# Two transformer blocks on one core: when the conditioning products of the second block are computed

## The chip, the core and the metric

The kernel runs on one core of a Trainium2 chip. The core has TensorE (PE: matmuls), VectorE (DVE), ScalarE (ACT), GpSimd (POOL) and SyncE (SP), which here only issues the transfers from HBM. The metric is the device time of one execution in microseconds, the median of several runs.

## What is computed

Both blocks have two layers, 256 tokens and 1024 channels. The first is a transformer with three mixing branches and a squared-ReLU MLP, the second a block of FFN, mixer, FFN, each behind a norm that is modulated by a conditioning vector `c`. That modulation is what the change is about:

```python
cond = jax.nn.silu(c)
for l in range(DEPTH):
    mod = cond @ ada_w[l] + ada_b[l]                 # 1024 -> 9 * 1024
    sh1, sc1, g1, sh2, sc2, g2, sh3, sc3, g3 = jnp.split(mod, N_MOD, axis=-1)
    hn = _modulate(_rms_norm(h, norm_g[l, 0]), sh1, sc1)
    h = h + 0.5 * g1[:, None, :] * _swiglu(hn, ffn1_w_in[l], ffn1_w_out[l])
    hn = _modulate(_rms_norm(h, norm_g[l, 1]), sh2, sc2)
    ...                                              # four mixers, joined as mixed
    h = h + g2[:, None, :] * (mixed @ w_out[l])
    hn = _modulate(_rms_norm(h, norm_g[l, 2]), sh3, sc3)
    h = h + 0.5 * g3[:, None, :] * _swiglu(hn, ffn2_w_in[l], ffn2_w_out[l])
```

## The kernel before

**Weights.** All matmul weights come in one list of chunks (`_plan`), each cut into pieces of 512 KB. SP loads a piece into one of five buffers `raw`; ACT rounds it to `wh`, DVE subtracts to get the rest `wl` (`split_to`), and PE does three matmuls per block of 128x128 (`mm3`). A piece is split three pieces ahead of its use, and loaded five ahead of its split. A piece of 1024 columns is 24 matmuls. A chunk of the FFNs is two pieces.

**Conditioning.** `cond @ ada_w[l]` isn't done on PE. Each layer has 72 columns of 128 values, 24 for each of the three norms (8 of shift, 8 of scale, 8 of gate). For each column a 512 KB slab of `ada_w` is loaded into one of two buffers `ada`, and one DVE instruction multiplies it by `cond` and sums along the row (`ada_step`). I call this a product. There are 144 of them. A step first issues the load for the next product, so that a load runs one product ahead. The DMA can start only when the product two before it has freed the buffer.

**When products go out.** `chunk` does `prog["ada"]` products at each weight chunk, a number that the stages set: 1 in the twelve gate chunks of both layers of the first block, 0 to 2 in its MLP, 1 in FFN1 of the second block's first layer, 2 in FFN2 of that layer. `ada_to(n)` does at once what is missing up to product n. When column 71 of a layer is there, the bias is added for all 72 columns, and `scl` and `hg` (scale and gate) are made for the three norms. All 144 products are done in the first FFN2.

**Who needs them.** Each norm's values are read first by `Shifted` (called by `following` near the end of the stage ahead): ACT rounds the shift columns of `mods` into the last columns of the tiles `xh`, DVE subtracts for the rest. In the mixer `following` stands behind the last token matmuls (`mv`) and ahead of the output projection (tile `mo`), whose input parts `mixh`, `mixl` are finished there: `fp` is a forget-attention softmax, `fpT` its transposed copy on ACT, `fo` the matmul on it, and `mixh`/`mixl` of `fo` the operand of the third and fourth `mo` piece.

**Order.** The program is written in one order, and a tile scheduler then orders each engine's queue; a queue is worked off in order. An instruction that waits holds everything behind it on its engine, on SP the transfers.

Of the kernel before, what the change touches and what calls it, by code (L numbers as in the profile page):

```python
# [15 lines left out]
ALU = mybir.AluOpType  # L16
# [5 lines left out]
L = 2  # L22
# [99 lines left out]
def tile_model(ctx: ExitStack, tc: tile.TileContext, xT: bass.AP, pos: bass.AP, cvec: bass.AP, wst: bass.AP,  # L122
               ada: bass.AP, vec: bass.AP, vec2: bass.AP, wsT: bass.AP, cst: bass.AP,
               msk: bass.AP, ret: bass.AP, outT: bass.AP):
    nc = tc.nc
# [15 lines left out]
    def const(shape, s, dt=F32):  # L141
        t = cp.tile(shape, dt, tag=s, name=s)
        return t
# [39 lines left out]
    def stt(out, in0, s, in1, op0, op1, **kw):  # L183
        nc.vector.scalar_tensor_tensor(out=out, in0=in0, scalar=s, in1=in1, op0=op0, op1=op1, **kw)  # L184
# [4 lines left out]
    def add(out, a, b):  # L189
        tt(out=out, in0=a, in1=b, op=ALU.add)  # L190
# [17 lines left out]
    for i, t in enumerate(subs):  # L208
        first_sub.setdefault(t[0], i)
    raws, split = {}, {}  # L210
    prog = {"raw": 0, "split": 0, "chunk": 0, "fill": 0, "turn": 0, "ada": 0}

    def load_to(s):
        while prog["raw"] < min(s, len(subs)):
# [7 lines left out]
    def split_to(s, ahead=5):  # L222
        while prog["split"] < min(s, len(subs)):
            i = prog["split"]
            load_to(i + ahead)
            _, _, n, cc, _ = subs[i]
            wh = wp.tile([P, SUB_COLS], F32R, tag="wh", bufs=4, name=nm("wh"))
            wl = wp.tile([P, SUB_COLS], F32R, tag="wl", bufs=4, name=nm("wl"))
            src = raws.pop(i)[:, :n * cc]
            nc.scalar.copy(wh[:, :n * cc], src)  # L230
            ins = tt(out=wl[:, :n * cc], in0=src, in1=wh[:, :n * cc].bitcast(F32), op=ALU.subtract)  # L231
            prog["dve"] = ins.ins
            split[i] = (wh, wl)
            prog["split"] += 1
# [3 lines left out]
    def fill():  # L238

        prog["fill"] += 1  # L240
        for g in list(bgs):
            if prog["fill"] >= due[g]:
                step(g)
# [12 lines left out]
    due = {}  # L256
# [8 lines left out]
    def chunk(key, l, k0, kk, c0, cc):  # L265
        j = prog["chunk"]
        assert plan[j] == (key, l, k0, kk, c0, cc), (plan[j], (key, l, k0, kk, c0, cc))
        prog["chunk"] += 1
        for _ in range(prog["ada"]):
            ada_step()  # L270
        s = first_sub[j]
        while s < len(subs) and subs[s][0] == j:
            split_to(s + 3)
            _, k, n, _, _ = subs[s]
            wh, wl = split.pop(s)
            for i in range(n):
                yield k0 + k + i, wh[:, i * cc:(i + 1) * cc], wl[:, i * cc:(i + 1) * cc]
            fill()
            s += 1
# [67 lines left out]
    def vc(n, i=0, k=1):  # L347
        return V[:, VC[n] + i:VC[n] + i + k]
# [165 lines left out]
    mods = [const([P, 72], f"mods{l}") for l in range(L)]  # L514
    scl = [const([P, 24], f"scl{l}") for l in range(L)]
    hg = [const([P, 24], f"hg{l}") for l in range(L)]
# [4 lines left out]
    def ada_load(upto):  # L521
        while ada_n[0] < min(upto, L * 72):
            i = ada_n[0]
            t = wp.tile([P, 1024], F32, tag="ada", bufs=2, name=nm("ada"))
            with tc.issue_after(prog["dma"]):
                nc.sync.dma_start(t, ada[i])
            ada_raw[i] = t
            ada_n[0] += 1

    def ada_step():  # L530
        i = ada_n[1]
        if i >= L * 72:
            return
        ada_n[1] += 1
        ada_load(i + 2)
        l, j = i // 72, i % 72
        w = ada_raw.pop(i)
        stt(w, w, 1.0, cond[0], ALU.mult, ALU.mult, accum_out=mods[l][:, j:j + 1])
        if j == 71:
            add(mods[l], mods[l], vc(f"adab{l}", 0, 72))  # L540
            for q in range(3):
                stt(scl[l][:, 8 * q:8 * q + 8], mods[l][:, 24 * q + 8:24 * q + 16], 1.0, vc(f"ng{l}", 8 * q, 8),
                    ALU.add, ALU.mult)
                nc.vector.tensor_scalar_mul(hg[l][:, 8 * q:8 * q + 8], mods[l][:, 24 * q + 16:24 * q + 24],
                                            1.0 if q == 1 else 0.5)

    def ada_to(n):
        while ada_n[1] < n:
            ada_step()
# [69 lines left out]
    for l in range(L):  # L619
# [27 lines left out]
        for i in range(5):  # L647
            src = b4[i // 2].t[:, (i % 2) * 256:(i % 2) * 256 + 256]
            hi_, lo_, j, g = (cqh, cql, i, "gq") if i < 3 else (ckh, ckl, i - 3, "gkv")
# [262 lines left out]
                    base_table(ins)  # L912
            return f

        prog["ada"] = 1
        for p in range(12):
            proj_pair(4352 + 256 * p, gate_e(p))

        prog["ada"] = 0
        mixed = [u4("mx") for _ in range(2)]  # L920
        mh = Act(8, "mh")
        for n, (y, gg) in enumerate(((ya, ga), (yb, gb), (yc, gc))):
# [45 lines left out]
        def hid_e(b, m):  # L968
# [3 lines left out]
            mul(q_, r_, r_)  # L972
            sub(hid.l(m, 2), q_, hid.h(m, 2).bitcast(F32))

        b4 = [Bank("u1", True) for _ in range(4)]
        gemm([("U", l, 2 * i, 2, 0, 1024) for i in range(4)], h.h, h.l, pair_outs(b4), 7, after={1: nrm2})
        for j in range(4):
# [2 lines left out]
        bd = [Bank("dn", True) for _ in range(4)]  # L980
        for half in range(2):
            for i in (range(4, 8) if half == 0 else range(8, 16)):
                prog["ada"] = min(2, i - 4)
                b = Bank("u2", half == 0)
                gemm([("U", l, 0, 8, 256 * i, 256)], h.h, h.l, pair_outs([b]), 7)
                hid_e(b, 2 * i)
            for m in range(4):
                prog["ada"] = 0 if half and m == 3 else 1
                gemm([("D", l, 8 * k, 8, 256 * m, 256) for k in (2 * half, 2 * half + 1)], hid.h, hid.l,
                     pair_outs([bd[m]]), 31)  # L990
                if half and l == 0:
                    update(m, bd[m], "full", rsm, "mix1", nh)
                elif half:
                    if m == 0:
                        ada_to(72)
                        mul(gfa, vc("final", 0, 8), scl[0][:, 0:8])
                        xa = Shifted(0, 0, lambda k: gfa[:, k:k + 1])
                    update(m, bd[m], "full", rsm)
                    xa.parts(m)
                    dst = t2("sqf")  # L1000
                    for e in range(2):
                        act(dst[:, e * 256:(e + 1) * 256], xk(2 * m + e), AF.Square, scale=vc("final", 2 * m + e))
                    accumulate(1, m, dst)
# [40 lines left out]
    def following(l, i):  # L1044
        l, i = (l, i + 1) if i < 2 else (l + 1, 0)
        if l == L:
            return None
        return Shifted(l, i, lambda k: scl[l][:, 8 * i + k:8 * i + k + 1])

    def gated_update(j, bank, l, i, nxt, part=None):  # L1050
# [15 lines left out]
    def ffn(l, f, i, xa, first=False):  # L1066
        h, r = Act(8, "h"), rcomb if first else rsx
        hid = Act(22, "hid")
        b4 = [Bank("f1", True) for _ in range(4)]
        nrm = normalised(h, l, i, first)  # L1070
        gemm_shift(("F" + f, l, 0, 8, 0, 512), xa, b4, lambda: next(nrm))
        for j in range(2):
            s_, q_ = t1("sg"), t1("sv")
            bg_, bu_ = b4[2 * j], b4[2 * j + 1]
            cg, cu = shift_bias(bg_), shift_bias(bu_)
            mul(s_, bg_.t[:, 0:256], r)
            act(s_, s_, AF.Silu, bias=cg)
            mul(q_, bu_.t[:, 0:256], r)
            stt(q_, q_, cu, s_, ALU.add, ALU.mult)
            hilo(q_, hid.h(j), hid.l(j))  # L1080
        for j in range(20):
            if j == 2:
                prog["ada"] = 1 if first else 2
            if first and j in range(2, 10):
                next(nrm)
            b = Bank("f2", True)
            gemm([("F" + f, l, 0, 8, 512 + 256 * j, 256)], h.h, h.l, pair_outs([b]), 7)
            s_, q_ = t1("sg"), t1("sv")
            ins = act(s_, b.t[:, 0:256], AF.Silu)
            mul(q_, s_, b.t[:, 256:512])  # L1090
            hilo(q_, hid.h(j + 2), hid.l(j + 2))
        if i == 2:
            ada_to(L * 72)
        nxt = following(l, i)
        base_table(ins)
        for m in range(4):
            if m == 2:
                prog["ada"] = 0
            b = Bank("fd", True)
            parts = [("G" + f, l, k, kk, 256 * m, 256) for k, kk in ((0, 8), (8, 8), (16, 6))]  # L1100
            if nxt is None and m == 3:
                gemm(parts[:2], hid.h, hid.l, pair_outs([b]), 21)
                parts = list(chunk(*parts[2]))
                for e in range(2):
                    for k, wh, wl in parts:
                        mm3(b, b.t[:, e * 256:e * 256 + 256], wh[:, e * P:(e + 1) * P], wl[:, e * P:(e + 1) * P],
                            hid.h(k), hid.l(k), k == 21)
                    gated_update(m, b, l, i, nxt, e)
            else:
                gemm(parts, hid.h, hid.l, pair_outs([b]), 21)  # L1110
                gated_update(m, b, l, i, nxt)
        return nxt
# [411 lines left out]
```

## Time and profile before

| | |
|---|---|
| median of 3 runs | 1986.65 us (1985.24 to 1990.67) |
| the profiled execution, its time | 1991.63 us |
| its span, first to last instruction | 1989.9 us |
| PE busy | 1948.8 us, 98% |
| DVE busy | 1485.2 us, 75% |
| granted TensorE clock, mean | 0.994 |

The profiled execution is 1.73 us longer than its span, and 4.98 us above the median of the runs. All times inside a run below are from the start of the span. PE's busy share is no measure of its pace, since matmuls overlap; where it waits is read from its waits, and what a stage takes from when the first matmul of a stage starts.

### The profile page before, as it was taken

The numbers are of one execution on the slowest core, as the hardware profiler recorded it, in microseconds if no ns is written. First come the engines' busy times: TensorE is split into PE (matmuls) and PEld (weight loads), VectorE is DVE, ScalarE is ACT, GpSimd is POOL, SyncE is SP. The second block draws the span as 40 slices with busy tenths as digits, with TensorE's granted clock in tenths as the row PEclk, the third lists the DMA queues.
The fourth block names the chain that finished last, engine by engine and source line by source line (L and its number), as shares of the span: only waits on it lengthen the run. The fifth ranks groups of instructions, "written<-read, shape, count | busy, mean of one in ns | idle before, by whom it ended". The sixth has DMA issues, their size and how long they took to land.

```text
span 1989.9 us, 38234 instructions
## 1 busy us (share of the span) xinstructions
PE 1948.8 (98%) x15570; PEld 1879.0 (94%) x15570; DVE 1485.2 (75%) x2329; ACT 1056.5 (53%) x1590; POOL 85.6 (4%) x86
## 2 busy tenths in 40 slices
PE   8999999999999999999999998999999999899999
PEld 7989999999989999999999986998999999789999
DVE  7878778796678777789877798888575558977553
ACT  5756555354556555455544466644454445665442
POOL 1000020001010010002000000000000000000000
PEclk9999999999999999999999998999999999999999
DMA  7545657896445656887677633388655554335554
GB/s 257 177 157 207 211 177 254 300 324 230 152 149 180 232 173 204 295 297 283 222 274 269 233 117 106 118 311 302 196 165 201 182 179 158 119 109 169 182 171 127
DMA packets 114945, 406.51 MB, mean 204 GB/s; under 512 B 12880, under 2 KB 14672, under 8 KB 114768
## 3 DMA queue, kind: packets, MB, share of 16 engines
q1 hardware_dynamic: 114768, 404.06, 60.3%
q8 instruction: 122, 2.00, 0.4%
q14 instruction: 55, 0.45, 0.1%
HBM read 402.96 MB, written 1.05 MB: 203 GB/s over the span
## 4 chain that ended last, share of the span: by engine, by line
PE 85%; DVE 9%; ACT 2%; issue 2%; DMA 1%; SPq 0%; POOL 0%; POOLq 0%; DVEq 0%; ACTq 0%
PE f L171 22%; PE fd L171 13%; PE pr L171 12%; PE u L171 9%; PE dn L171 9%; PE br L171 3%; DVE wl L231 2%; PE wo L171 2%; DVE cv L184 2%; PE a L171 1%; PE mo L171 1%; PE sbv L171 1%; PE rv L171 1%; PE uq L171 1%; PE z L171 1%
## 5 line engine op out<-in xcount | busy, mean ns | idle before, releaser
L230 ACT CAST wh<-raw 128x1024 fp32r<-128x1024 f32 (+1 forms) x627 | 642.8, 1030 | 662.7 <-PE fd L171 118.0
L231 DVE TENSOR_TENSOR wl<-raw,wh 128x1024 fp32r<-128x1024 f32 (+1 forms) x627 | 756.0, 1211 | 318.2 <-ACT wh L230 316.4
L171 PE MATMUL f<-hh,wl 128*128 128x256 f32 x1280 | 362.2, 283 | 3.1 <-DVE wl L231 3.1
L171 PE MATMUL f<-hl,wh 128*128 128x256 f32 x1280 | 362.3, 283 | 0.8 <-DVE hl L193 0.8
L171 PE MATMUL f<-hh,wh 128*128 128x256 f32 x1280 | 362.2, 283 | 0.8 <-ACT wh L230 0.6
L171 PEld LDWEIGHTS f<-hh,wl 128*128 128x128 f32 x1280 | 245.4, 192 | 4.4 <-DVE wl L231 4.4
L171 PEld LDWEIGHTS f<-hh,wh 128*128 128x128 f32 x1280 | 245.6, 192 | 1.4 <-ACT wh L230 1.4
L171 PEld LDWEIGHTS f<-hl,wh 128*128 128x128 f32 x1280 | 245.7, 192 | 1.2 <-DVE hl L193 1.2
L184 DVE SCALAR_TENSOR_TENSOR ada<-ada,cond 128x1024 f32<-128x1024 f32 x144 | 176.6, 1227 | 70.6 <-DMA ada<-ada_dram 70.2
L171 PE MATMUL fd<-hidh,wh 128*128 128x256 f32 x704 | 199.3, 283 | 0.6 <-DVE x L184 0.6
L171 PE MATMUL fd<-hidl,wh 128*128 128x256 f32 x704 | 199.2, 283 | 0.0
L171 PE MATMUL fd<-hidh,wl 128*128 128x256 f32 x704 | 199.2, 283 | 0.0
L171 PE MATMUL pr<-hh,wh 128*128 128x256 f32 x672 | 194.8, 290 | 0.0
L171 PE MATMUL pr<-hl,wh 128*128 128x256 f32 x672 | 190.0, 283 | 0.0
L171 PE MATMUL pr<-hh,wl 128*128 128x256 f32 x672 | 190.0, 283 | 0.0
L171 PE MATMUL u<-hh,wh 128*128 128x256 f32 x512 | 145.2, 284 | 0.0
L171 PE MATMUL dn<-hidh,wl 128*128 128x256 f32 x512 | 145.0, 283 | 0.0
L171 PE MATMUL u<-hh,wl 128*128 128x256 f32 x512 | 145.0, 283 | 0.0
L171 PE MATMUL dn<-hidh,wh 128*128 128x256 f32 x512 | 144.9, 283 | 0.0
L171 PE MATMUL dn<-hidl,wh 128*128 128x256 f32 x512 | 144.9, 283 | 0.0
L171 PE MATMUL u<-hl,wh 128*128 128x256 f32 x512 | 144.9, 283 | 0.0
L171 PEld LDWEIGHTS fd<-hidh,wh 128*128 128x128 f32 x704 | 135.2, 192 | 0.8 <-DVE x L184 0.8
(475 smaller groups left out, 4452.0 us busy)
## 6 DMA issues: line engine op xcount, KB each, us to landing
raw<-wst_dram SPq DMA_DIRECT2D x599, 512.0 KB, 3.9
ada<-ada_dram SPq DMA_DIRECT2D x144, 512.0 KB, 5.2
raw<-wst_dram SPq DMA_DIRECT2D x22, 256.0 KB, 2.8
raw<-wst_dram SPq DMA_DIRECT2D x4, 390.0 KB, 3.0
R<-ret_dram SPq DMA_DIRECT2D x2, 512.0 KB, 8.9
out_dram<-x SPq DMA_DIRECT2D x8, 128.0 KB, 3.1
C<-cst_dram SPq DMA_DIRECT2D x1, 896.0 KB, 7.1
v<-vec_dram SPq DMA_DIRECT2D x2, 448.0 KB, 4.6
```

The lines of the kernel that those rows point to most:

```text
L171: nc.tensor.matmul(out, lhsT=lhsT, rhs=rhs, start=grp not in self.open, stop=stop, skip_group_check=True)
L184: nc.vector.scalar_tensor_tensor(out=out, in0=in0, scalar=s, in1=in1, op0=op0, op1=op1, **kw)
L230: nc.scalar.copy(wh[:, :n * cc], src)
L231: ins = tt(out=wl[:, :n * cc], in0=src, in1=wh[:, :n * cc].bitcast(F32), op=ALU.subtract)
```

## The change

The bias, `scl` and `hg` are now made for each norm as soon as its 24 columns are there. `prog["ada"]` may be a fraction: what is due is added up per chunk, and a product goes out when it reaches one. The gate chunks send out none; the chunks of the first block's up projection send one in two, FFN1 and FFN2 of the second block one per chunk in both layers. What a norm still lacks when `Shifted` is about to read it is done at once by `ada_to` in `following`.

```diff
@@ chunk
-        for _ in range(prog["ada"]):
+        prog["due"] += prog["ada"]
+        while prog["due"] >= 1.0:
+            prog["due"] -= 1.0
             ada_step()
@@ ada_step
-        if j == 71:
-            add(mods[l], mods[l], vc(f"adab{l}", 0, 72))
-            for q in range(3):
...
+        if j % 24 == 23:
+            q = j // 24
+            mq = mods[l][:, 24 * q:24 * q + 24]
+            add(mq, mq, vc(f"adab{l}", 24 * q, 24))
...
@@ first block
-        prog["ada"] = 1
         for p in range(12):
             proj_pair(4352 + 256 * p, gate_e(p))
 
-        prog["ada"] = 0
...
+        prog["ada"] = 0.5
         b4 = [Bank("u1", True) for _ in range(4)]
...
-                prog["ada"] = min(2, i - 4)
+                prog["ada"] = 0.5
...
-                        ada_to(72)
+                        ada_to(24)
@@ following
+        ada_to(72 * l + 24 * (i + 1))
         return Shifted(l, i, lambda k: scl[l][:, 8 * i + k:8 * i + k + 1])
@@ ffn
-            if j == 2:
-                prog["ada"] = 1 if first else 2
+            prog["ada"] = 1
...
-        if i == 2:
-            ada_to(L * 72)
```

Counted from the program by the loads, which run one product ahead: 45 stand in the first block, 26 in the first layer's FFN1, 2 in the first mixer (where `ada_to` asks for what is missing of the first layer), 24 in the first FFN2 up to its `following` (the last 4 by `ada_to`), 32 from there to the end of the second layer's FFN1, and the last 15 in the second mixer, where `ada_to(144)` asks for everything that is left.

DVE in the second layer's mixer, between the second part of the mix (`mixl` from `co`) and the operand from `fo`. Before:

```order
L193 TENSOR_TENSOR mixl_19813<-co_20648,mixh_19811 128x512
L611 RECIPROCAL rc_20686<-fs_20680 128x2
...
L595 TENSOR_REDUCE mx_20696<-fs_20666 128x1
L193 TENSOR_TENSOR xh_20711<-mods_161,xh_20711 128x3
...
L231 TENSOR_TENSOR wl_20839<-raw_20578,wh_20838 128x1024
...
L231 TENSOR_TENSOR wl_20881<-raw_20619,wh_20880 128x1024
L1247 COPY do_20807<-do_20802 128x256
L193 TENSOR_TENSOR mixl_19812<-fo_20811,mixh_19810 128x256
```

The same place in the changed kernel, from the last free stretch on:

```order
L184 SCALAR_TENSOR_TENSOR ada_20684,mods_161<-ada_20684,cond_1820 128x1024
L231 TENSOR_TENSOR wl_20885<-raw_20574,wh_20884 128x1024
L184 SCALAR_TENSOR_TENSOR ada_20687,mods_161<-ada_20687,cond_1820 128x1024
L184 SCALAR_TENSOR_TENSOR ada_20690,mods_161<-ada_20690,cond_1820 128x1024
...
L184 SCALAR_TENSOR_TENSOR ada_20705,mods_161<-ada_20705,cond_1820 128x1024
L184 SCALAR_TENSOR_TENSOR ada_20708,mods_161<-ada_20708,cond_1820 128x1024
L190 TENSOR_TENSOR mods_161<-mods_161,V 128x24
L184 SCALAR_TENSOR_TENSOR scl_163<-mods_161,V 128x8
...
L193 TENSOR_TENSOR xh_20715<-mods_161,xh_20715 128x3
...
L193 TENSOR_TENSOR mixl_19767<-fo_20815,mixh_19765 128x256
```

Before, the stretch had no products. Now the fifteen tiles ada_20666 to ada_20708 (numbers in steps of three) are worked off here: the first ahead of the softmax of `fs`, two just ahead of `mixl` from `co`, twelve behind it, the last eight with nothing between them. `mixl` from `fo` stands behind all of them.

ACT at the same place. The names are those of the section on the kernel; `wh` is a rounded weight piece. Before:

```order
L404 CAST xh_20711<-mods_161 128x3
...
L230 CAST wh_20838<-raw_20578 128x1024
...
L584 COPY fpT_20761<-tr_20762 128x384
L584 COPY fpT_20761<-tr_20767 128x384
L230 CAST wh_20880<-raw_20619 128x1024
```

And now:

```order
L230 CAST wh_20884<-raw_20574 128x1024
L1244 ACTIVATE dsq_20812<-do_20806 128x256
L406 CAST xh_20715<-mods_161 128x3
L406 CAST xh_20716<-mods_161 128x3
L406 CAST xh_20717<-mods_161 128x2
L585 COPY fpT_20765<-tr_20766 128x384
L585 COPY fpT_20765<-tr_20771 128x384
L202 CAST mixh_19765<-fo_20815 128x256
```

The three casts of the shift columns wait for `mods` with its bias, so for the last product. The copies `fpT` that the matmul `fo` reads stand right behind them.

SP at the same place, in the changed kernel (before, there are only `raw` loads here):

```order
L528 DMA ada_20684<-ada_dram 128x1024
L218 DMA raw_20882<-wst_dram 128x1024
L528 DMA ada_20687<-ada_dram 128x1024
L528 DMA ada_20690<-ada_dram 128x1024
L218 DMA raw_20924<-wst_dram 128x1024
L528 DMA ada_20693<-ada_dram 128x1024
...
L528 DMA ada_20708<-ada_dram 128x1024
L218 DMA raw_20954<-wst_dram 128x1024
```

Each of these `ada` loads waits on DVE for the buffer that the product two before it held; the weight loads stand between and behind them.

## Rows read from the trace of the kernel before

**Rows 1.** The page, busy time of the engines.
```profile
PE 1948.8 (98%) x15570; PEld 1879.0 (94%) x15570; DVE 1485.2 (75%) x2329; ACT 1056.5 (53%) x1590; POOL 85.6 (4%) x86
```
**Rows 2.** The chain of waits, one weight piece: start, duration.
```profile
86.77 2.87 PE pr L171 x24
```
**Rows 3.** The page's groups: busy, mean ns | idle before, releaser.
```profile
L184 DVE SCALAR_TENSOR_TENSOR ada<-ada,cond 128x1024 f32<-128x1024 f32 x144 | 176.6, 1227 | 70.6 <-DMA ada<-ada_dram 70.2
```
**Rows 4.** Waits of PE, first FFN2 (1269 to 1405): total, times, longest.
```profile
PE f L171 <- DVE wl L231: 2.9, 4, 0.8
PE f L171 <- ACT wh L230: 0.6, 1, 0.6
```
**Rows 5.** Waits of PE, second FFN2's first half (1790 to 1922).
```profile
PE nrm L171 <- POOL ssum L371: 1.9, 1, 1.9
```
**Rows 6.** Timeline of PE, first matmuls of f and fd: start, duration, instruction.
```profile
1269.19 0.28 PE L171 MATMUL f<-xh,wh 128*128 128x258 f32 x1
...
1404.81 0.28 PE L171 MATMUL fd<-hidh,wh 128*128 128x256 f32 x1
...
1790.32 0.28 PE L171 MATMUL f<-xh,wh 128*128 128x258 f32 x1
...
1922.02 0.28 PE L171 MATMUL fd<-hidh,wh 128*128 128x256 f32 x1
```
**Rows 7.** A stretch of the first layer's gate chunks: busy by engine, clock, DMA share, GB/s.
```profile
136.00:234.00 98.00, 98.00 (x817) 93.02 (x816) 78.54 (x126) 57.87 (x87) 0.00 (x0) 1.00 0.62 215
```
**Rows 8.** Timeline of DVE, one product in the first FFN2.
```profile
1350.82 1.23 DVE L184 SCALAR_TENSOR_TENSOR ada<-ada,cond 128x1024 f32<-128x1024 f32 x1 [1.14 <-DMA ada<-ada_dram]
1351.97 0.08 DVE L184 DVE_READ_ACCUMULATOR ada<-ada,cond 128x1 f32 x1
```
**Rows 9.** Timeline of SP, behind that product, and in the second mixer.
```profile
1352.09 0.33 SPq L526 DMA_DIRECT2D ada<-ada_dram  x1
...
1744.51 4.01 SPq L218 DMA_DIRECT2D raw<-wst_dram  x4
```
**Rows 10.** The tile ada: its 144 loads.
```profile
DMA to landing us min/median/max: 3.2/5.2/8.3
```
**Rows 11.** DMA issues from 1800 to 1920: count, size, median us to landing.
```profile
raw<-wst_dram SPq DMA_DIRECT2D x40, 512.0 KB, 3.3
```
**Rows 12.** Timeline of DVE, second mixer, last parts.
```profile
1750.95 0.17 DVE L611 RECIPROCAL rc<-fs 128x2 f32<-128x2 f32 x1 [0.44 <-ACT fp L597]
...
1763.29 0.69 DVE L193 TENSOR_TENSOR mixl<-co,mixh 128x512 fp32r<-128x512 f32 x1 [2.76 <-ACT mixh L202]
1764.87 0.17 DVE L611 RECIPROCAL rc<-fs 128x2 f32<-128x2 f32 x1 [0.88 <-ACT fp L597]
...
1765.92 0.35 DVE L193 TENSOR_TENSOR xh<-mods,xh 128x3 fp32r<-128x3 f32 x3
1767.05 1.23 DVE L231 TENSOR_TENSOR wl<-raw,wh 128x1024 fp32r<-128x1024 f32 x1 [0.78 <-ACT wh L230]
```
**Rows 13.** Timeline of DVE, the bias of the second layer.
```profile
1385.52 0.23 DVE L190 TENSOR_TENSOR mods<-mods,V 128x72 f32<-128x72 f32 x1
```
**Rows 14.** Timeline of ACT, second mixer.
```profile
1765.65 0.42 ACT L404 CAST xh<-mods 128x3 fp32r<-128x3 f32 x3
...
1767.95 0.91 ACT L584 COPY fpT<-tr 128x384 f32<-128x384 f32 x2
```
**Rows 15.** Timeline of PE, second mixer.
```profile
1769.39 0.82 PE L171 MATMUL fo<-fpT,vt 128*64 128x256 f32 x8
...
1772.91 0.47 PE L171 MATMUL mo<-mixl,wh 128*128 128x256 f32 x1
```
**Rows 16.** PE by stretches: length, busy, clock, DMA share, GB/s.
```profile
1738.00:1742.00 4.00, 3.17 (x8) 0.57 0.41 131
1752.00:1756.00 4.00, 4.00 (x15) 0.57 0.14 55
```
**Rows 17.** Waits of PE, first FFN1 (945 to 1077).
```profile
PE f L171 <- DVE hl L193: 0.8, 2, 0.6
```

More of the change, by code (lines that the diff above doesn't have):

```diff
@@ L210, in tile_model @@
     raws, split = {}, {}
-    prog = {"raw": 0, "split": 0, "chunk": 0, "fill": 0, "turn": 0, "ada": 0}
+    prog = {"raw": 0, "split": 0, "chunk": 0, "fill": 0, "turn": 0, "ada": 0.0, "due": 0.0}
     def load_to(s):
@@ L538, in ada_step @@
         stt(w, w, 1.0, cond[0], ALU.mult, ALU.mult, accum_out=mods[l][:, j:j + 1])
-        if j == 71:
-            add(mods[l], mods[l], vc(f"adab{l}", 0, 72))
-            for q in range(3):
[L542 to L545, printed above, removed]
+        if j % 24 == 23:
+            q = j // 24
+            mq = mods[l][:, 24 * q:24 * q + 24]
+            add(mq, mq, vc(f"adab{l}", 24 * q, 24))
+            stt(scl[l][:, 8 * q:8 * q + 8], mq[:, 8:16], 1.0, vc(f"ng{l}", 8 * q, 8), ALU.add, ALU.mult)
+            nc.vector.tensor_scalar_mul(hg[l][:, 8 * q:8 * q + 8], mq[:, 16:24], 1.0 if q == 1 else 0.5)
     def ada_to(n):
```

## The prediction

> **What bounds the kernel now.** I read the page's busy times first: PE 98%, DVE 75% [rows 1]. PE's busy share is no pace, so the waits of PE came next, and they are short. The kernel is a stream of weight pieces at 2.87 us each [rows 2], and nothing that a change does on DVE is felt unless PE has to wait for it. So the question is where the products make PE wait now, and where they will.
>
> Now they do so at one place. The group row puts a product at 1227 ns and DVE's idle time ahead of products at 70.6 us [rows 3], but in most stages PE doesn't feel it. In the first FFN2, with two products per chunk, PE waits 2.9 us for `wl` and 0.6 us for `wh` [rows 4]; the same stage of the second layer, without products, has neither [rows 5], and the wait for `nrm` is the same in both. The stage heads say the same with the restarts in it: from the first `f` to the first `fd` it takes 1404.81 − 1269.19 = 135.62 us in the first layer and 1922.02 − 1790.32 = 131.70 us in the second [rows 6]. All that the spreading can give back is the difference, 3.9 us. Taking the products out of the gate chunks gives nothing: of 98 us there PE is busy for all 98 [rows 7].
>
> **What the change adds: the second mixer.** The count in the program leaves 15 loads for the `ada_to(144)` in the second layer's mixer, and DVE, ACT and SP are each worked off in order. Three things then hang on the last product: on DVE the operand `mixl` from `fo`, on ACT the casts of the shift columns with the copies `fpT` behind them, and through these on PE the matmul `fo`. On SP one weight load stands behind the last six `ada` loads, but its buffer is only freed by a `wl` that comes after the products, so it costs nothing by itself. Nothing in PE's queue can go on past `fo`.
>
> How long do the products take? With two buffers they go round: a product with its read-out lasts 1351.97 + 0.08 − 1350.82 = 1.23 us [rows 8], the next load into its buffer goes out at 1352.09, 0.04 us later [rows 9], and when it has landed the buffer's next product can run. For the landing the rows differ. The 144 loads of `ada` took 3.2 to 8.3 us, median 5.2 [rows 10], but these had weight loads issued just ahead of them. Weight loads of the same size that come singly, one per piece, took 3.3 us [rows 11]. In the mixer the weight buffers are full and two `ada` loads alternate, so I take 3.3, with 3.2 and 5.2 as the ends. A turn of two products is 1.23 + 0.04 + 3.3 = 4.57 us.
>
> The Trainium skill has a price for a load as well: "DMA: Bandwidth & Descriptors", section "Anatomy of one DMA", gives a fixed 2.0 us and the bytes over 436 GB/s, which for 512 KB is an estimate of 3.2 us. The trace agrees in its minimum and not in its median. By that price six turns are 0.6 us shorter than by mine.
>
> Now the places, on the clock of the trace before. The first of the fifteen is loaded right behind the weight load at 1744.51 [rows 9] and its product falls where DVE waits 0.44 us ahead of 1750.95 [rows 12]. The second and third are loaded by then or soon after, and fall into the 2.76 us ahead of `mixl` from `co` at 1763.29 [rows 12]: that wait hides them. The second starts 2.6 us ahead of that, at 1760.7, and ends at 1761.9; from there its buffer goes round. Twelve products are left, six turns: the eleventh ends at 1761.9 + 6 × 4.57 = 1789.3, the twelfth follows directly, at least 1.23 us and with its issue some 1.5 us later, 1790.8. Other work stands between the first ones: the softmax's five small instructions, 1.05 us from 1764.87 to 1765.92, two `wl` of 1.23 us, and a few copies [rows 12]. Followed product by product, the turns hide most of it and 1.8 us stay: 1792.6. The bias is 0.23 us [rows 13], so `mods` is there at about 1792.9.
>
> Then the chain starts: casts 0.42 us, the copies `fpT` 0.91 us [rows 14], and two hand-overs of about 0.1 us, so `fo` starts at 1794.5 and not at 1769.39 [rows 15], 25.1 us late. From `fo` to the free stream of `mo` the trace before takes 3.5 us, to 1772.91 [rows 15], with `mixh` and `mixl` in it; that stays, but the four matmuls of the next piece that ran between aren't done yet, 0.5 us. So PE loses 25.6 us. Ends by the landing: 0.6 less at 3.2 us, and 6 × 1.9 = 11.4 more at 5.2 us.
>
> **The clock behind the wait.** In this mixer PE has short waits, and behind them the granted clock is 0.57 over 4 us, twice: at full busy from 1752 to 1756 and nearly so from 1738 to 1742 [rows 16]. That is mostly the lower of its two levels, 1.2 GHz, and costs 0.43 × 4 = 1.7 us each. A wait of 25 us isn't in the trace, so I take one such stretch, 1.7 us; ends nothing (it falls into the chain from `fo` on, which waits for ACT and DVE anyway) and twice as much.
>
> **The smaller places.** (a) The end of the first FFN2: four forced products and the next ones come with the last weight pieces, eight products at about one per piece, the density that costs 3.9 us over 26 products in the same stage now; 3.9 × 8/26 = 1.2 us. Ends: nothing, or 8 × (3.27 − 2.87) = 3.2 us if every product took half a turn with loads of 5.2 us, (5.2 + 1.27 + 0.07)/2 = 3.27 us, against the 2.87 of a piece. (b) The first mixer: one product on the path of `sg` and the softmax, 1.23 us against a wait of 0.44 as in the second mixer; 0.8 us, ends nothing and 2.2 us. (c) FFN1 of the second layer takes 26 products at one per chunk. FFN1 of the first layer carries that now and has no wait for `wl` or `wh`, only 0.8 us for `hl` at its start [rows 17], so nothing. (d) `scl`, `hg` and the bias now run six times and not twice, on eight to 24 columns: 0.2 us each, hidden, as DVE waits at those places.
>
> **The sum.** −3.9 + 25.6 + 1.7 + 1.2 + 0.8 = +25.4 us. Against the profiled execution, 1991.63 us, that is 2017.0 us. The median of the runs is 4.98 us below that execution, so I forecast 1986.65 + 25.4 = 2012 us. Its own range: down by 0.6 + 1.7 + 1.2 + 0.8 = 4.3 us, and some 4 us for the spread of the runs, to 2004; up by 11.4 us and the spread, to 2025.
>
> **The rivals.**
> 1. The loads in the mixer take 5.2 us, as `ada` loads mostly do now [rows 10], for instance since the two weight loads between them go along. For it: that is their median over 144. Against: those medians come from stages in which a weight load goes out with every product, and here there are two weight loads to fifteen. Price 11.4 us more: 2023.5 us.
> 2. The end of the first FFN2 becomes a second stall. There too the casts of the shift columns stand on ACT, ahead of four roundings `wh`, and wait for the last forced product. PE has three split pieces, 8.6 us, in hand; a load of 5.2 us and two products take 7.7 us, so it just holds. If it doesn't, pieces are late by one or two turns: 8 us more, 2020 us.
> 3. The products wait for no load: DVE does them back to back, 1.5 us each. Twelve are then 18 us and the other work between them 5, from 1761.9 to 1784.5; `mods` comes 8 us sooner and the result is 2004 us. Against: with two buffers a load must land between.
> 4. The other side: the mixer hides the products, and only the gain of the first FFN2 is left, 1986.65 − 3.9 + 2.0 for the small places = 1985 us, or 1983 without these. It decides on DVE, at the cast: `mods` must be there by 1768, when `fpT` is copied now [rows 14]. Twelve products in the 6 us from 1761.9 is 0.5 us each, under half of what one takes on DVE [rows 8]. Only an order of the queues other than the built one could do it.
>
> That the change does not do what its words say is in the forecast: one product per chunk is too few to be done in time, and the rest isn't spread but forced.
>
> **Chances.** Forecast 0.71, rival 1 0.15, rival 2 0.07, rival 3 0.03, rival 4 0.03, and 0.01 for no change. A measurement of this kernel can tell 0.3%, 6 us, from no change; all but the last two are slower by more, so slower 0.96, same 0.01, faster 0.03. The range of 8 in 10, 2004 to 2025 us, holds the forecast with its bounds and rivals 1 and 2 for the most part.
>
> **What would show it.** In the profile after: PE waiting for ACT's `fpT` at `fo` in the second mixer for 20 us or more in one piece, with DVE waiting for DMA `ada` ahead of eight products in a row; starts of products some 4.6 us apart by pairs; no waits for `wl` in the middle of the first FFN2; a granted clock well under 1 in the few us behind the wait. It would be wrong if `fo` were less than 15 us late, if the loads there took over 5 us, or if PE had a further wait of several us at the end of the first FFN2 or in the second layer's FFN1.

## The result and the profile after

| | before | after |
|---|---|---|
| median of the runs | 1988.18 us (4 runs, 1985.24 to 1990.67) | 2012.22 us (4 runs, 2010.59 to 2013.56) |
| the profiled execution, its span | 1991.63, 1989.9 us | 2010.59, 2008.8 us |
| granted TensorE clock, mean | 0.994 | 0.991 |

The median before was of three runs where the change is described; a fourth, 1989.72 us, makes it 1988.18. The ratio is 1.0116 [1.0103, 1.0129]: slower by 24 us. The busy times hardly changed, which is the first thing to see on the page after; beside [rows 1] only the shares moved, since the span is longer:

```profile
PE 1945.1 (97%) x15570; PEld 1876.6 (93%) x15570; DVE 1491.7 (74%) x2333; ACT 1058.5 (53%) x1590; POOL 83.7 (4%) x86
```

The waits of PE over the whole run (total, times, longest) name the place. Their first line has no counterpart before; nothing else there is of its size:

```profile
PE fo L171 <- ACT fpT L585: 25.4, 1, 25.4
PE mv L171 <- DVE wl L231: 6.7, 6, 2.4
```

The longest of before is the second of these:

```profile
PE mv L171 <- DVE wl L231: 6.7, 6, 2.5
```

DVE in the second mixer after, behind [rows 12] (start, duration, instruction, idle before and its releaser). The rows left out are products of the same kind and a few small ones:

```profile
1755.31 0.69 DVE L193 TENSOR_TENSOR mixl<-co,mixh 128x512 fp32r<-128x512 f32 x1 [0.48 <-ACT mixh L202]
1757.00 1.23 DVE L184 SCALAR_TENSOR_TENSOR ada<-ada,cond 128x1024 f32<-128x1024 f32 x1 [1.00 <-DMA ada<-ada_dram]
...
1764.16 1.22 DVE L184 SCALAR_TENSOR_TENSOR ada<-ada,cond 128x1024 f32<-128x1024 f32 x1 [0.17 <-DMA ada<-ada_dram]
...
1782.20 1.23 DVE L184 SCALAR_TENSOR_TENSOR ada<-ada,cond 128x1024 f32<-128x1024 f32 x1 [1.26 <-DMA ada<-ada_dram]
...
1784.69 1.22 DVE L184 SCALAR_TENSOR_TENSOR ada<-ada,cond 128x1024 f32<-128x1024 f32 x1 [1.25 <-DMA ada<-ada_dram]
...
1785.95 0.18 DVE L190 TENSOR_TENSOR mods<-mods,V 128x24 f32<-128x24 f32 x1
...
1789.34 0.42 DVE L193 TENSOR_TENSOR mixl<-fo,mixh 128x256 fp32r<-128x256 f32 x1 [2.59 <-ACT mixh L202]
```

From 1757.00 on there are twelve products. Eight of them start after 1764.16, over 20.53 us, so 2.57 us each: a product of 1.22 us and then a wait for its load (once with a `wl` before that wait). At 1785.95 the bias is added, and ACT, idle since 1762.0, goes on at once (ACT's timeline, against [rows 14]):

```profile
1786.17 0.39 ACT L406 CAST xh<-mods 128x3 fp32r<-128x3 f32 x3 [24.14 <-DVE mods L190]
1786.46 0.85 ACT L585 COPY fpT<-tr 128x384 f32<-128x384 f32 x2
```

PE's timeline at the heads of the two FFN2 and at `fo`, against [rows 6, 15]:

```profile
1267.03 0.28 PE L171 MATMUL f<-xh,wh 128*128 128x258 f32 x1
...
1398.95 0.28 PE L171 MATMUL fd<-hidh,wh 128*128 128x256 f32 x1
...
1786.98 1.92 PE L171 MATMUL fo<-fpT,vt 128*64 128x256 f32 x8 [25.40 <-ACT fpT L585]
...
1810.88 0.28 PE L171 MATMUL f<-xh,wh 128*128 128x258 f32 x1
...
1940.99 0.28 PE L171 MATMUL fd<-hidh,wh 128*128 128x256 f32 x1
```

`fo` takes 1.92 us for eight matmuls that took 0.82. The stretches say why (length, busy PE, PEld, DVE, ACT, POOL, clock, DMA share, GB/s):

```profile
1764.00:1785.00 21.00, 0.00 (x0) 0.00 (x0) 11.32 (x18) 0.00 (x0) 0.00 (x0) 0.52 0.69 238
1785.00:1788.00 3.00, 1.02 (x5) 0.78 (x7) 1.68 (x8) 1.14 (x5) 0.00 (x0) 0.50 0.00 0
1788.00:1792.00 4.00, 4.00 (x17) 2.29 (x13) 0.42 (x1) 1.33 (x3) 0.00 (x0) 0.50 0.00 0
1792.00:1796.00 4.00, 4.00 (x32) 3.57 (x31) 0.42 (x1) 0.67 (x2) 0.00 (x0) 0.98 0.00 0
```

PE does nothing for 21 us, and then runs at the lower level, 1.2 GHz, until about 1792, in which time the second half of `fo` and of the mix is late too.

Stage by stage, taken from first matmul to first matmul in the two profiled executions: start and first block −0.7; first FFN1 −0.5; first mixer −0.9 (129.23 to 128.29); first FFN2 −3.7 (135.62 to 131.92); second layer's FFN1 0.0; second mixer +26.4 (130.36 to 156.78); last FFN2 −1.6. With −0.1 behind it that is +18.9, the difference of the spans.

### The profile page after: what moved, and what is told of

Same layout as the page of the kernel before. It is cut to its first block, busy times and chain, and to the rows that moved or that the text cites. A ratio compares the mean times of both kernels' runs of the same rounds, so it can differ in the third digit from the quotient of the medians.

```text
span 2008.8 us, 38193 instructions
## 1 busy us (share of the span) xinstructions
PE 1945.1 (97%) x15570; PEld 1876.6 (93%) x15570; DVE 1491.7 (74%) x2333; ACT 1058.5 (53%) x1590; POOL 83.7 (4%) x86
## 4 chain that ended last, share of the span: by engine, by line
PE 85%; DVE 10%; ACT 2%; DMA 2%; issue 1%; SPq 0%; POOL 0%; POOLq 0%; DVEq 0%; ACTq 0%
PE f L171 24%; PE fd L171 12%; PE pr L171 12%; PE dn L171 9%; PE u L171 9%; PE br L171 3%; PE wo L171 2%; DVE wl L231 2%; DVE cv L184 2%; PE a L171 1%; PE mo L171 1%; PE sbv L171 1%; PE rv L171 1%; DMA ada<-ada_dram 1%; PE uq L171 1%
```

## The experiments

**Theory A.** What `ada_to(144)` must still do in the second mixer goes round two buffers, about 2.5 us per product, and PE pays for all that the mixer's own waits don't hide. Three rivals: the place of the request decides and not the number; the products as such are too much there, loads or not; or the handling per norm costs something by itself.

**1. The gate chunks send products too** (on top of the changed kernel):

```diff
+        prog["ada"] = 1
         for p in range(12):
             proj_pair(4352 + 256 * p, gate_e(p))
+        prog["ada"] = 0
```

> The changed kernel, but the twelve gate chunks of each layer send out one product each again (rate 1), so that all 144 products are out in the second layer's FFN1 and nothing is forced in the second mixer. Theory A (the loss is the 15 forced loads and products in the second mixer, 28 us with the slow clock behind them, and the spreading itself costs nothing): 1983 to 1986 us, 2 to 5 us under the kernel before, and no wait of PE on fpT over 1 us. Rival B (one product per chunk in the second layer's FFN1 and the smaller places cost, or the finer groups do): over 1990 us.

Measured: 1984.64 us (8 runs, 1982.63 to 1986.42), ratio to before 0.9971 [0.9959, 0.9984]. The last product starts at 1602.2 us, ahead of the second mixer, and no wait for `fpT` is left. The first half of the first FFN2, from `f` to `fd`, takes 130.32 us, and its only wait is the one for `nrm`, as in [rows 5]. So the change with products in the gate chunks, and with none forced in the second mixer, is a gain of 0.3%, small but clear of its interval.

**2. The last twelve loads left out.** The products stay and read an old slab, so the last columns of `mods` are not those of the reference.

```diff
-        while ada_n[0] < min(upto, L * 72):
+        while ada_n[0] < min(upto, 132):
...
-        w = ada_raw.pop(i)
+        w = ada_raw.pop(i) if i < 131 else ada_raw[131]
```

> The changed kernel, with the loads of the last 12 products left out; these 12 use the slab that is there, so the last columns of the second layer's modulation are wrong. The products themselves stay where they are. Theory A1 (the loads' round trip through two buffers sets the pace, 2.5 us per product): products follow each other at 1.2 to 1.5 us, mods is ready 9 to 12 us sooner, 2000 to 2004 us. Rival A2 (DVE's own time for 15 products and what stands between sets it): no more than 3 us faster, 2009 us or more.

Measured: 2000.11 us (1999.77 to 2002.08), ratio 1.005 [1.0032, 1.0068]. The wait, from the waits of PE:

```profile
PE fo L171 <- ACT fpT L585: 13.8, 1, 13.8
```

The last five products now start 1.27 us apart. Of the 25.4 us, 11.6 are the round trips of these twelve loads; the other 13.8 are the products on DVE and what stands between them, which nothing hides.

**3. `following` moved behind the output projection's loop**, so that the casts and with them `ada_to(144)` are asked for later:

```diff
-        nxt = following(l, 1)
         ...
+        nxt = following(l, 1)
```

> The changed kernel, with the mixer's call of following moved behind the first three quarters of the output projection, so that neither fpT on ACT nor mixl of fo on DVE stands behind the products. Theory A1 (the forced products last 25 us longer than PE has work that doesn't need them): the wait moves to the head of FFN2 and stays, 2007 to 2016 us. Rival A3 (the loss comes from the place, the casts ahead of fpT in ACT's queue): most of it goes, 1990 to 1998 us.

Measured: 2020.65 us (2019.04 to 2022.44), ratio 1.0155 [1.0133, 1.0176]. This was above the expected range. The wait left `fo` and came back at the next stage, longer:

```profile
PE f L171 <- ACT xh L417: 33.7, 1, 33.7
```

The fifteen products start 1776.8 to 1816.5, 2.8 us apart, so the first comes 34 us later than in the changed kernel (1743.0). The three that the softmax's waits had hidden are in the open as well, and PE has only some 21 us of its own work (`fo` to `f`) ahead of the point where it needs them. The place is not what is wrong; asking later only takes cover away.

**4. Only the handling per norm**, in the kernel before, with its numbers of products:

```diff
-        if j == 71:
-            add(mods[l], mods[l], vc(f"adab{l}", 0, 72))
...
+        if j % 24 == 23:
+            q = j // 24
+            mq = mods[l][:, 24 * q:24 * q + 24]
+            add(mq, mq, vc(f"adab{l}", 24 * q, 24))
...
```

> The kernel before with one part of the change alone: bias, scl and hg per norm, in groups of 24. The rates and places of the products are those of before. Theory A: no difference, ratio 0.998 to 1.002. Rival B (the finer groups cost, as they put small instructions into busy stretches of DVE): 2 us or more slower.

Measured: 1987.54 us (12 runs), ratio 0.9988 [0.9979, 0.9998]. The six small groups in place of two cost nothing; the loss doesn't come from this part of the change.

**5. No products at all.** This is experiment 1 with all 144 loads and products left out and `mods` filled with a constant, so the conditioning is not computed:

```diff
-        ada_load(i + 2)
...
-        w = ada_raw.pop(i)
-        stt(w, w, 1.0, cond[0], ALU.mult, ALU.mult, accum_out=mods[l][:, j:j + 1])
+        if i % 72 == 0:
+            nc.vector.memset(mods[l], 0.01)
```

> The version with gate products (e1, 1984.6 us) with all 144 loads of ada_w and all 144 products left out; mods is filled with a constant, so the conditioning is not computed. Theory: what products cost is the waits that they put into PE's stream, and in e1 these are nearly gone, so leaving the products out altogether gives 1981 to 1986 us, at most 3 us less than e1. Rival: DVE's 180 us of products and 72 MB of loads slow the whole stream a little everywhere (weight loads that land late, DVE late by a fraction); then it is 1978 us or less.

Measured: 1982.87 us (7 runs, 1981.57 to 1985.54), ratio 0.9973 [0.9962, 0.9984], beside 0.9971 [0.9959, 0.9984] with all products. In experiment 1 the 177 us of products and 72 MB of loads are therefore hidden as far as this can be measured, and nothing that can be measured is left to gain from moving them.

**6 and 7. The dose.** As experiment 1, but with fewer products in the gate chunks: 12 more than in the changed kernel, which leaves 9 forced ones, and 18 more, which leaves 3. The first of the two lines is in experiment 6, the second in 7:

```diff
+        prog["ada"] = 1 if l else 0
...
+        prog["ada"] = 1 if l else 0.5
```

> The changed kernel, with one product per chunk in the second layer's gate chunks again (12 more products early). That leaves 9 instead of 15 loads for the second mixer; three still fall into the waits there. Theory: the wait at fo is the ring of two buffers, 2.5 us per forced product, so it falls from 25.4 by 6 x 2.5 = 15 us to about 10 us, and the time to 1995 to 1999 us. Rival: the wait is the place (the casts behind the bias) more than the count; then it stays over 15 us and the time over 2001 us.

> The changed kernel, with one product per gate chunk in the second layer and one per two in the first (18 more products early). That leaves 3 loads for the second mixer, as many as its waits hide. Theory: the wait at fo is under 2 us and the time 1983 to 1989 us, as with all gate products. Rival: any product forced in the mixer delays the bias and the casts; then fo is 3 to 8 us late and the time 1988 to 1994 us.

Measured: 1997.4 us (1996.04 to 1998.83), ratio 1.0048 [1.0034, 1.0062]; and 1984.52 us (10 runs, 1981.91 to 1988.59), ratio 0.9985 [0.9974, 0.9995]. With 9 forced products the wait of PE is

```profile
PE fo L171 <- ACT fpT L585: 10.2, 1, 10.2
```

and with 3 there is none, for the three products lie at 1743.34, 1752.98 and 1754.12, in the places where the mixer waits anyway. Six products are 25.4 − 10.2 = 15.2 us, 2.5 us each; by that slope the wait would end at five. That is Theory A with its number; the rivals of both expectations are out.

**8. PE kept busy during the wait**, to see whether the slow stretch behind it is the clock: 112 matmuls without use ahead of `fo`.

```diff
+            if l == 1 and i == 0:
+                for _ in range(112):
+                    nc.tensor.matmul(b_o.t, lhsT=idle[:, 0:P], rhs=idle, start=True, stop=True, skip_group_check=True)
```

> The changed kernel with 112 more matmuls of 128x512 (results unused) in PE's queue just ahead of fo in the second layer's mixer, so that PE is busy for most of the 25 us in which it waits for the products. Theory: what is lost behind the wait is the granted clock, 0.50 from 1785 to 1792 us in the changed kernel; with PE busy the clock stays at 1.00, from fo to the first f of FFN2 it takes 21 to 21.6 us and not 23.9, and the time is 2 to 3 us less, 2009 to 2010.5 us. Rival: that stretch is longer for the chain from mods over ACT and DVE, not for the clock; then the time stays at 2012 us and the stretch at 23.9.

Measured: 2010.3 us (2009.85 to 2013.72), ratio 1.0118 [1.0101, 1.0136]. PE's timeline (the view starts inside the idle matmuls and shows the last 60), and the stretch behind the wait:

```profile
1775.82 13.54 PE L1289 MATMUL fo<-idle 128*128 128x512 bf16 x60
1789.30 0.87 PE L171 MATMUL fo<-fpT,vt 128*64 128x256 f32 x8
...
1810.38 0.28 PE L171 MATMUL f<-xh,wh 128*128 128x258 f32 x1
```

```profile
1788.00:1792.00 4.00, 3.99 (x29) 2.36 (x28) 0.64 (x4) 2.01 (x6) 0.00 (x0) 1.00 0.00 0
```

The clock stays at 1.00, `fo` is back at 0.87 us, and from `fo` to `f` it takes 21.08 us and not 23.90. So in this execution these 2.8 us are the clock's. In the time they can't be seen: `fpT` was ready at about 1788.4, and the idle matmuls, which ended at 1789.36, held `fo` up by 0.9 us; the rest went to products that ended 1.5 us later than in the changed kernel's profile.

**9. Half-size loads.** The last twelve loads bring 512 of 1024 columns, and GpSimd fills the rest with zeros (so the last twelve columns of `mods` are half sums):

```diff
+                if i >= 132:
+                    nc.sync.dma_start(t[:, 0:512], ada[i][:, 0:512])
+                    nc.gpsimd.memset(t[:, 512:1024], 0.0)
```

> The changed kernel with the last 12 loads of ada_w half as large (512 of 1024 columns; GpSimd fills the rest with zeros, so the last 12 conditioning columns are sums over half the slab). The products on DVE keep their size. Theory: a turn of the ring is 1.27 us of product and a landing that is part transfer: over 1764 to 1785 us of the changed kernel 238 GB/s at a DMA share of 0.69 are 345 GB/s at full share, 1.52 us for 512 KB. Half the bytes take 0.76 us off each landing and 0.38 us off each of some 11 products: the wait at fo is 20.5 to 22 us, the time 2007 to 2009 us. Rival 1: the landing is nearly all fixed time; then the wait stays over 24 us. Rival 2: the two loads under way slow each other; then the landing falls by 1.2 us or more and the wait to 18 us or less.

Measured: 2006.84 us (2004.2 to 2010.98), ratio 1.0087 [1.0064, 1.0111]. The wait of PE, and the landing of the mixer's `ada` loads, three of which are still whole:

```profile
PE fo L171 <- ACT fpT L589: 22.2, 1, 22.2
```

```profile
DMA to landing us min/median/max: 2.5/3.1/5.6
```

The wait is just above the 20.5 to 22 us and lies between the rivals' bounds of 18 and 24; the time is just below its range. Against the two executions of the changed kernel (25.4, and 26.2 in experiment 11) half the bytes save 3 to 4 us. The median landing of the twelve loads alone is 2.9 us here and 3.7 in the changed kernel: half the bytes take off 0.8 us, so the larger part of a landing doesn't go with the bytes. The Trainium skill ("DMA: Bandwidth & Descriptors", section "Anatomy of one DMA", which is written for transfers issued by GpSimd; here SP issues them) gives a fixed 2.0 us and the bytes over 436 GB/s, an estimate of 2.6 us for 256 KB and 3.2 for 512 KB; the minima agree, 2.5 here and 3.2 in the changed kernel, and the medians, 3.1 and 3.8, lie above.

**10 and 11. Fewer idle matmuls, beside the changed kernel once more.** `range(104)` in place of `range(112)`, and the changed kernel unaltered, timed on one chip.

> As the kernel with 112 idle matmuls ahead of fo, with 104 of them, 8 x 0.213 = 1.7 us less: with 112 they ended 0.9 us after fpT was there and held fo up by that. Theory: fo starts when fpT is there, the clock is still 1.00 behind it, fo to the first f takes 21 to 21.5 us, and the time is 2.0 to 3.0 us less than that of the changed kernel timed beside it. Rival: the clock falls anyway in the last us without work, or the time lost behind the wait was not the clock; then it is within 1 us of the changed kernel.

> The changed kernel itself once more, for the comparison with the idle matmuls on one chip: 2010.5 to 2013.6 us, ratio 1.011 to 1.013, and a wait of 25 to 26 us at fo. If its profiled run has fo to f at 23.9 us again, the lower clock behind the wait is there in every run; if it is 21 to 22, it is one of the stretches that vary from run to run.

Measured: 2011.39 us (2006.87 to 2015.9), ratio 1.0109 [1.0091, 1.0128], and 2011.06 us (2010.2 to 2012.34), ratio 1.0109 [1.0092, 1.0126]. So experiment 10 missed: no gain. Its profiled execution is the slowest of its five. There the last product came at 1789.69, PE had run out of idle matmuls and waited after all, and the clock fell again:

```profile
1791.98 1.92 PE L171 MATMUL fo<-fpT,vt 128*64 128x256 f32 x8 [3.26 <-ACT fpT L585]
```

```profile
1792.00:1796.00 4.00, 4.00 (x20) 2.93 (x22) 0.42 (x1) 1.64 (x4) 0.00 (x0) 0.61 0.00 0
```

The changed kernel again has its wait, 26.2 us (just above the 25 to 26 expected), and 1811.53 − 1787.94 = 23.6 us from `fo` to `f`. The slow stretch belongs to the wait. What it would give back if PE were kept busy is shown for the stretch in one execution, and isn't shown for the time.

## Why the prediction held

The forecast was 2012 us, and 2012.22 was measured, with the mechanism, the place and the waiting engine as foretold. That the time agrees to 0.2 us is luck: the forecast put 25.4 us on a median of three runs, 1986.65, and the difference of the medians of four is 24.0; and several terms missed in opposite directions. Step by step:

**The wait at `fo`.** Forecast 25.1 us late. From the mixer's token matmuls on, the first `mv` starts at 1718.17 after and at 1725.53 before; with these 7.36 us taken off, `fo` is 1786.98 + 7.36 − 1769.39 = 24.95 us late. The number is better than its parts: from 1764.16 on two products took 20.53/4 = 5.13 us and not 4.57 (the one `wl` among them ended 0.95 us before the next load was there). The landing was 3.8 us in the median, and 3.7 in the twelve loads that go round, not 3.3 as the single weight loads of [rows 11] had suggested (the loads of the fifteen products in the mixer):

```profile
DMA to landing us min/median/max: 3.2/3.8/6.0
```

Against that, the second product of the mixer came at 1752.47, 0.9 us sooner than forecast, and the first turns, which have the softmax and two `wl` in them, were not longer than the others: from 1757.00 to 1764.16 three products took 2.39 us each. The 1.8 us charged for that work were hidden in the landings. The forecast has 4.57 us and 0.3 of other work per turn, 4.87; from the second product's end to the eleventh's it was (1783.4 − 1753.7)/6 = 4.95. Two terms at the end missed by about a microsecond each and cancel too: the last product was to end 1.5 us behind the one before it and ended 2.5 us behind, for it also waited for its load (1.25 us in the lines above), and from `mods` to `fo` it took 0.85 us and not 1.6.

**Behind the wait.** Forecast 0.5 us for matmuls not yet done and 1.7 for the clock, 2.2; measured 23.90 − 20.93 = 2.97 us from `fo` to `f`. Experiment 8 gives all but 0.2 of it to the clock, so the clock's term was too small (2.8 us, not 1.7) and that of the matmuls too large. The stretch at the lower level was longer than the one of [rows 16]: 0.50 from 1785 to 1792. Among the long waits its cost doesn't grow with the wait: after 10.2, 13.8 and 22.2 us (experiments 6, 2 and 9) it takes 23.95, 23.84 and 23.72 us from `fo` to `f`.

**The first FFN2.** Forecast −3.9, measured −3.7. The waits for `wl` and `wh` of [rows 4] are gone, as forecast; what is left in that stage is the line of [rows 5]:

```profile
PE nrm L171 <- POOL ssum L373: 1.9, 1, 1.9
```

That the sizes agree is luck. Behind this wait the granted clock fell in some executions and not in others, with the wait 1.9 us in each, and the fall makes the stage some 1.6 us longer. The stretches behind it in the first FFN2, before, after, and in the second execution of the changed kernel (experiment 11):

```profile
1277.00:1281.00 4.00, 4.00 (x36) 4.00 (x35) 3.90 (x10) 1.60 (x3) 0.00 (x0) 1.00 0.81 254
1275.00:1279.00 4.00, 4.00 (x29) 4.00 (x29) 3.36 (x8) 1.71 (x3) 0.00 (x0) 0.79 0.91 292
1277.00:1281.00 4.00, 4.00 (x36) 4.00 (x35) 3.90 (x10) 1.75 (x3) 0.00 (x0) 1.00 0.82 298
```

The forecast subtracted 131.70 us, of a stage in which the clock had fallen (the last FFN2 before, next lines), from 135.62, of one in which it hadn't. With the clock at 1.00 the changed kernel takes 1399.14 − 1268.78 = 130.36 us, so taking out the doubled products is worth 5.3 us and not 3.9; the profiled execution after had the fall, and so shows 3.7.

**The last FFN2.** It had no term and came out 1.6 us shorter, for the clock fell there before and not after:

```profile
1798.00:1802.00 4.00, 4.00 (x28) 4.00 (x27) 3.18 (x7) 1.73 (x3) 0.00 (x0) 0.77 0.74 259
1819.00:1823.00 4.00, 4.00 (x36) 4.00 (x35) 3.90 (x11) 1.67 (x2) 0.00 (x0) 1.00 0.73 241
```

This one doesn't look like scatter: the seven profiled executions in which `fo` came late (after, experiments 2, 6 and 8 to 11) all take 130.1 us from `f` to `fd`, and the five in which it didn't (before, experiments 1, 4, 5 and 7) 131.7. Why is open. Experiment 3, with its wait at the head of this stage, can't be compared.

**The small places.** The end of the first FFN2 was to cost 1.2 us, and its second half takes 63.36 us after and 63.35 before: the nine products that ran there cost nothing, so pricing them by the density of the stage ahead was wrong. The first mixer was to cost 0.8 us and came out 0.9 shorter, but that doesn't show the product to be free: the clock alone gave 2.0 us in the stretch from the first matmul into `gu` to the first `mv` (14.32 us before, 12.30 after; see the last section), and from there to `f` it is 64.21 us after and 63.14 before. The versions with a product there take 63.2 to 64.2 us for this, those without one 63.1 to 64.8, so what it costs can't be told. The 26 products in the second layer's FFN1 cost nothing (191.79 us for the whole stage, before 191.80), as forecast.

**From terms to time.** The sum was +25.4 us on a profiled execution of 1991.63, carried over to the medians. The medians differ by 24.0, the two profiled executions by 19.0. The 5.1 us between are in the choice of executions: that of before was 3.45 us above the median of its four runs (4.98 above that of three), and that of after, the fastest of four, 1.63 below. In the stages 3.5 us of this stand in `gu` of the two mixers, 14.32 and 13.79 us before and 12.30 both times after. The last section shows what such executions differ in.

Three slips in the working changed nothing: 4 us of spread on top of 2012 + 11.4 is 2027 and not 2025; rival 3's products end at 1761.9 + 18 + 5 = 1784.9 and not 1784.5; and in (a) the 0.07 us are in no row, without them 8 × (3.24 − 2.87) = 2.9 us.

**The rivals.** Slow landings of 5.2 us, a stall at the end of the first FFN2 and products back to back didn't come about; experiment 2 is the third of these made by hand, with 2000 us where 2004 was worked out. The rival in which the mixer hides the products was priced at 1983 to 1985 us, and experiments 1 and 7 reached that, 1984.6 and 1984.5, with products sent early enough.

The version of experiment 1 beats both kernels: 0.9971 [0.9959, 0.9984] of the time before.

## What to carry to other kernels

Spreading background work evenly is worth it only if all of it is done before the first reader: count what is left at the point where the program asks for the rest, and price each piece at the round trip of its buffers (here 2.5 us for 1.2 us of work), not at its busy time. A rest as large as the waits of that place hide is free (three products were; by the slope of experiment 6 up to five), and each one more is paid in full on the engine that waits. More than two buffers, or asking for the rest at the start of the mixer, weren't tried. Where an in-order queue holds a small instruction that needs the last piece, what counts is what stands behind it: here three casts kept back two copies, and these PE.

## What was not expected of the hardware

The same short wait is sometimes followed by a drop of the granted clock and sometimes not, in two executions of one program. In the first mixer of the changed kernel, the matmuls into `gu` take 12.30 us in one profiled execution and 14.38 in the other. Stretches of PE in the first one (columns as above):

```profile
1190.00:1194.00 4.00, 3.62 (x23) 2.41 (x22) 4.00 (x10) 3.06 (x9) 0.00 (x0) 1.00 0.41 131
1194.00:1198.00 4.00, 3.81 (x29) 3.11 (x27) 4.00 (x10) 1.04 (x1) 0.00 (x0) 1.00 0.44 134
```

And in the second:

```profile
1190.00:1194.00 4.00, 3.63 (x26) 2.59 (x24) 4.00 (x11) 3.48 (x11) 0.00 (x0) 1.00 0.40 131
1194.00:1198.00 4.00, 4.00 (x22) 3.83 (x23) 4.00 (x10) 0.00 (x0) 0.00 (x0) 0.62 0.39 132
```

PE's busy time in the first four us is the same to 0.01 us, and then the clock is 1.00 in one and 0.62 in the other, with 29 matmuls done against 22. PE's wait just ahead, for `qu`, is 0.35 us in both. Over all profiled executions of this study this stage takes, in either mixer, 12.3 us or 12.8 to 15.3. The wait for `nrm` in the first FFN2, shown above, is a second such place. Such a drop is about 2 us, a part of the 2 to 9 us by which runs of one kernel, timed together, differ here, and it makes a difference of 5 us between two profiled executions no finding by itself.

The landings of the loads in the ring scatter too: medians of 3.8 and 4.2 us in two executions of the changed kernel, with 15 loads each. What sets them isn't settled here, beyond that half the bytes save 3 to 4 us over twelve loads.
